# Two transformer blocks on one core: the split weight tiles get eight starting places in SBUF instead of one

## The chip, the cores and the metric

The kernel runs on one core of a Trainium2 chip (trn2). The metric is the device time of one execution in microseconds. Three executions of the kernel before took 2203.39, 2204.60 and 2204.74 us; their median is 2204.6 us.

## What is computed

Two blocks follow one another on a sequence of 256 tokens with 2048 channels, all in fp32. The first mixes a gated convolution, a pooling branch and a cross-attention to a memory of 256 tokens, and has a convolved feed-forward part; the second has a dilated and a differential attention and a feed-forward part. Nearly all the work is products of the activations with weights:

```python
def first_block(x, mem, ...):
    z = rmsnorm(x, g_mix) @ w_in                 # 2048 -> 3584, split in five
    ...                                          # conv, pooling, cross-attention
    x = x + concat([conv_out, pool_out, att]) @ w_out
    u = causal_dwconv(rmsnorm(x, g_ffn) @ w_up, ffn_conv_w) + ffn_conv_b   # 2048 -> 2 x 5632
    gate, val = split(u)
    x = x + (silu(gate) * val) @ w_down          # 5632 -> 2048
    return rmsnorm(x, g_final)

def second_block(x, ...):
    qa, ka, va, qb, kb, vb = split(rmsnorm(x, norm_attn) @ w_in)           # 2048 -> 6144
    ...                                          # two attentions of 8 heads each
    x = x + concat([ya, yb]) @ w_out
    h = rmsnorm(x, norm_ffn)
    x = x + (silu(h @ w_gate) * (h @ w_up)) @ w_down
    return rmsnorm(x, norm_final)
```

## The kernel before

**Weights in two parts.** Each fp32 number is split into two fp32r numbers: `hi` is the rounded value and `lo` the rest. A product of weight w and activation x is made as w_hi·x_hi + w_hi·x_lo + w_lo·x_hi. The activations lie as [128 channels, tile number, 512]: the 256 tokens' hi values and behind them their 256 lo values. So one weight block of 128x128 costs two matmuls: a long one, 512 columns wide, with the block's hi part as the stationary operand (`long`, L206), and a short one, 256 columns wide, with its lo part (`short`, L209). `products` runs up to four blocks at once and joins neighbouring groups, so that in steady work eight longs and eight shorts take turns. In what follows a block means one long and one short.

**Units.** The weights come in units of 16 blocks, [128, 2048] fp32, in the order of use. `prefetch` loads a unit into a `raw` tile (pool `wraw`, three tiles of 8192 bytes a partition) three units ahead. ScalarE rounds one half of it at a time into a `hi` tile (`split_hi`, L173), VectorE takes the difference into a `lo` tile (`split_lo`, L185). A half is called a part and has the number j; it holds 8 blocks in 1024 columns, 4096 bytes a partition. There are four `hi` and four `lo` tiles, used in turn. `emit_all` writes out the order by hand: per stage of four blocks it issues the prefetch, the splits, the epilogues that are due (`posts`) and then the matmuls.

**Two forms of product.** Most units run in the form above, weights stationary and activations moving (`ws_units`). For the value projections the roles are exchanged (`vs_unit`, L273 to L275): the activations' parts are stationary (128 columns of A or M), and 512 columns of a `hi` or `lo` tile are moving; there are 480 such matmuls, all 512 wide.

**Which activations.** The moving tile is `A` for the projections that start from a normalised x (`w_in`, `w_up`, gate and up, q and k), and one tile of the tag `mix` for the others: `M` (the memory, only in the first 60 us), `mix`, `hid` (the hidden values of the feed-forward part) and `y`, which lie in the same bytes one after another. 14 small blocks take theirs from the pool `qk`.

**Where tiles lie.** A pool has its place in each partition's SBUF behind the pools that were opened before it. In the order of opening, with bytes a partition: `cst`, `wraw` (3 x 8192), `whi` (4 x 4096), `wlo` (4 x 4096), `big`, `t1` (14 x 1024), `qk` (6 x 2048), `t2` (4 x 2048), and small ones. `big` holds, in the order in which its tags are first made: `X` (16384), `A` (32768), `stg` (16448, which is 16 + 16·256 floats), `mix` (32768), and four tiles of 1024 for norms. All of these sizes from `wraw` on are multiples of 512 except that of `stg`, which is 64 over one. A 128-column weight block is 512 bytes long and an activation tile's row 2048 bytes.

Of the kernel before, what the change touches and what calls it, by code (L numbers as in the profile page):

```python
# [11 lines left out]
F32R = mybir.dt.float32r  # L12
# [6 lines left out]
P = 128  # L19
# [80 lines left out]
def tile_two_blocks(ctx: ExitStack, tc: tile.TileContext, a: dict, out: bass.AP):  # L100
    nc = tc.nc
    pool = lambda name, bufs, **kw: ctx.enter_context(tc.tile_pool(name=name, bufs=bufs, **kw))
    cst = pool("cst", 1)
    wraw_p = pool("wraw", 3)
    whi_p = pool("whi", 4)
    wlo_p = pool("wlo", 4)
    big = pool("big", 1)
    t1 = pool("t1", 14)
    qk_p = pool("qk", 6)
    t2 = pool("t2", 4)  # L110
    pl_p = pool("pl", 1)
    sm = pool("sm", 4)
# [40 lines left out]

    raws = {}
    halves = {}
    HB = UB * P // 2

    def prefetch(i):
# [6 lines left out]
    def split_hi(j):  # L165

        i, second = divmod(j, 2)
        c0 = HB * second
        if i >= len(units) or c0 >= units[i][1]:
            return  # L170
        n = min(units[i][1] - c0, HB)
        hi = whi_p.tile([P, HB], F32R, tag="hi", name=f"hi{j}")
        nc.scalar.activation(hi[:, :n], raws[i][:, c0:c0 + n], AF.Copy)  # L173
        halves[j] = (hi, None)

    def split_lo(j):

        i, second = divmod(j, 2)
        c0 = HB * second
        if i >= len(units) or c0 >= units[i][1]:  # L180
            return
        n = min(units[i][1] - c0, HB)
        hi = halves[j][0]
        lo = wlo_p.tile([P, HB], F32R, tag="lo", name=f"lo{j}")
        nc.vector.tensor_tensor(out=lo[:, :n], in0=raws[i][:, c0:c0 + n], in1=hi[:, :n].bitcast(F32), op=ALU.subtract)  # L185
        halves[j] = (hi, lo)

# [293 lines left out]
    def load_mem(k0, k1):  # L481
        c = slice(KT + k0 * S if k0 else 0, KT + k1 * S)
        nc.sync.dma_start(stg[:, c], a["mem"][:, c])

    def first_units():

        n = 4 * P
        for i in range(3):
            raws[i] = wraw_p.tile([P, UB * P], F32, tag="raw", name=f"raw{i}")
            for q in range(4):  # L490
                if i != 1:
                    load_mem(2 * i + q, 2 * i + q + 1)
                nc.sync.dma_start(raws[i][:, q * n:(q + 1) * n], units[i][0][:, q * n:(q + 1) * n])

        warm = m_p.tile([P, 512], F32, tag="m", name="warm")
        for _ in range(9):
            nc.tensor.matmul(warm[:, :P], lhsT=ones, rhs=ones, start=True, stop=True)
        for j in range(4):
            hi = whi_p.tile([P, HB], F32R, tag="hi", name=f"hi{j}")
            lo = wlo_p.tile([P, HB], F32R, tag="lo", name=f"lo{j}")  # L500
            for q in range(2):
                c = slice(q * n, (q + 1) * n)
                r = raws[j // 2][:, (j % 2) * HB + q * n:(j % 2) * HB + (q + 1) * n]
                nc.scalar.activation(hi[:, c], r, AF.Copy)
                if j < 2:
                    mem_act(2 * j + q)
                nc.vector.tensor_tensor(out=lo[:, c], in0=r, in1=hi[:, c].bitcast(F32), op=ALU.subtract)
            halves[j] = (hi, lo)
# [32 lines left out]
    def mem_act(kt):  # L541
        x, g, hi = mem_t[:, kt, :], gm[:, kt:kt + 1], M[:, kt, :S]
        nc.vector.tensor_scalar(out=hi, in0=x, scalar1=g, scalar2=None, op0=ALU.mult)
        nc.vector.scalar_tensor_tensor(out=M[:, kt, S:], in0=x, scalar=g, in1=hi.bitcast(F32),
                                       op0=ALU.mult, op1=ALU.subtract)
# [183 lines left out]
    for m in LAST_TILES:  # L729
        if m < 18:  # L730
            last_blocks += full_blocks([m], act_movs, 0)
        else:
            j, ins = POOL_PAIRS[m - 18]
# [273 lines left out]
    def emit_all():  # L1007
        nc.vector.memset(ones, 1.0)
        first_units()
        n = len(units)  # L1010
        for t in range(4 * n):
            i, q = divmod(t, 4)
            if q == 0:
                prefetch(i + 3)
            if q == 2:
                split_hi(2 * i + 4)
            stage(t)
            if q == 0 and i:
                split_lo(2 * i + 2)
                split_hi(2 * i + 3)  # L1020
            elif q == 1 and i:
                split_lo(2 * i + 3)
            units[i][2](i, q)
            for fn in extras.pop(t, ()):
                fn()
        t = 4 * n
        while posts or extras or running:
            stage(t)
            for fn in extras.pop(t, ()):
                fn()  # L1030
            t += 1
        finish()
# [96 lines left out]
```

## Time and profile before

| | |
|---|---|
| median of three executions | 2204.6 us (2203.39 to 2204.74) |
| the profiled execution, its own time | 2204.54 us |
| span of its instructions, first to last | 2202.7 us |
| mean granted TensorE clock | 0.996 of 2.4 GHz |
| TensorE matmuls busy | 2182.8 us (99%), 12426 |
| TensorE weight loads busy | 1909.5 us (87%), 12426 |
| VectorE busy | 1603.5 us (73%) |
| ScalarE busy | 1143.2 us (52%) |

The profile has a page (busy times, the chain of work that ended last) and answers from the trace (groups of instructions by line and shape, a timeline in order of time, who waited for whom). A matmul's recorded length overlaps that of the next one, since matmuls are pipelined; what a matmul costs in a row of like ones is therefore read from the starts: the start of a run, the start of the next run, and the number of matmuls between them.

### The profile page before, as it was taken

The page shows a single profiled execution, that of the slowest core. Times are in us where ns is not written, and L with a number is a line of the kernel's source. Part 1 is how long each engine was busy: PE and PEld are TensorE (multiplying, and loading weights), DVE is VectorE, ACT ScalarE, POOL GpSimd, SP SyncE. Part 2 cuts the span into 40 slices and gives each one's busy share as a digit, 9 for nine tenths or more (in the row PEclk, how much of TensorE's full clock was granted, in tenths as well). Part 3 has the DMA queues.
Part 4 walks back from the last instruction along what each step waited for, and adds up shares of the span by engine and source line. Part 5 has one row for each costly group of instructions (what it writes and reads, how often), then busy time and mean ns, then how long its engine had stood idle before and what let it go on. Part 6 is the DMA issues. An engine that isn't in the chain of part 4 may idle for free.

```text
span 2202.7 us, 31334 instructions
## 1 busy us (share of the span) xinstructions
PE 2182.8 (99%) x12426; PEld 1909.5 (87%) x12426; DVE 1603.5 (73%) x2553; ACT 1143.2 (52%) x1738; POOL 106.7 (5%) x114
## 2 busy tenths in 40 slices
PE   8999999999999999999999999999999999999997
PEld 7888888888888888888888888888888888888886
DVE  8877778886588757878779677786665666666666
ACT  6555556564465536565456655464443444344442
POOL 4000010000000000003100000010000000000012
PEclk9999999999999999999999999999999999999998
DMA  7545555555555555555544444555555555555553
GB/s 285 197 169 177 191 188 193 189 192 191 191 191 186 190 182 192 188 192 188 194 167 158 161 165 153 179 203 186 185 186 192 191 189 191 191 192 186 185 184 115
DMA packets 60195, 408.99 MB, mean 186 GB/s; under 512 B 6672, under 2 KB 8592, under 8 KB 11792
## 3 DMA queue, kind: packets, MB, share of 16 engines
q1 hardware_dynamic: 60048, 406.99, 53.9%
q8 instruction: 97, 1.59, 0.3%
q14 instruction: 50, 0.41, 0.0%
HBM read 404.86 MB, written 2.10 MB: 185 GB/s over the span
## 4 chain that ended last, share of the span: by engine, by line
PE 97%; DVE 1%; DMA 1%; issue 0%; SPq 0%; ACT 0%; DVEq 0%; ACTq 0%
PE acc L206 60%; PE acc L209 31%; PE acc L273 1%; PE acc L274 1%; PE acc L275 1%; PE s_ps L430 1%; DVE lo L185 0%; DMA X<-in_x 0%; PE pT_ps L466 0%; PE o_ps L920 0%; PE o_ps L878 0%; DMA raw<-in_w_k 0%; DVE end L998 0%; PE nps L342 0%; PE o_ps L638 0%
## 5 line engine op out<-in xcount | busy, mean ns | idle before, releaser
L173 ACT ACTIVATE hi<-raw 128x1024 fp32r<-128x1024 f32 x758 | 799.2, 1057 | 583.2 <-PE acc L206 413.9
L185 DVE TENSOR_TENSOR lo<-raw,hi 128x1024 fp32r<-128x1024 f32 x758 | 933.5, 1239 | 145.4 <-ACT hi L173 133.4
L206 PE MATMUL acc<-A,hi 128*128 128x512 f32 x3776 | 961.6, 394 | 0.0
L206 PEld LDWEIGHTS acc<-A,hi 128*128 128x128 f32 x3776 | 677.3, 189 | 119.8 <-issue 1.0
L209 PEld LDWEIGHTS acc<-A,lo 128*128 128x128 f32 x3776 | 518.5, 190 | 39.2 <-issue 0.7
L209 PE MATMUL acc<-A,lo 128*128 128x256 f32 x3776 | 535.0, 283 | 0.0
L206 PE MATMUL acc<-hid,hi 128*128 128x512 f32 x1408 | 360.2, 392 | 0.0
L206 PEld LDWEIGHTS acc<-hid,hi 128*128 128x128 f32 x1408 | 250.6, 188 | 41.5
L414 ACT ACTIVATE z<-acc 128x256 f32<-128x256 f32 x244 | 91.8, 382 | 274.2 <-PE acc L206 274.1
L209 PEld LDWEIGHTS acc<-hid,lo 128*128 128x128 f32 x1408 | 195.3, 188 | 17.2
L209 PE MATMUL acc<-hid,lo 128*128 128x256 f32 x1408 | 199.6, 279 | 0.0
L740 DVE TENSOR_TENSOR X<-acc,X 128x256 f32<-128x256 f32 x128 | 54.0, 422 | 177.4 <-PE acc L206 177.3
L416 DVE TENSOR_TENSOR z<-acc,z 128x256 f32<-128x256 f32 x244 | 103.0, 422 | 103.4 <-ACT z L414 102.6
L715 DVE SCALAR_TENSOR_TENSOR c<-z,vec,c 128x255 f32<-128x255 f32 (+1 forms) x188 | 90.0, 480 | 5.1 <-ACT c L710 1.2
L404 DVE TENSOR_TENSOR hid<-hid 128x256 fp32r<-128x256 f32 x88 | 37.4, 425 | 77.1 <-ACT hid L402 77.1
L422 DVE TENSOR_TENSOR z<-z,R_ffn 128x256 f32<-128x256 f32 x176 | 74.7, 424 | 6.0
L206 PE MATMUL acc<-y,hi 128*128 128x512 f32 x256 | 65.4, 394 | 0.0
L206 PE MATMUL acc<-mix,hi 128*128 128x512 f32 x256 | 64.2, 392 | 0.0
L317 POOL TENSOR_TENSOR sq_attn<-sq_attn,sqt 128x256 f32<-128x256 f32 x30 | 29.4, 993 | 707.9 <-ACT sqt L315 707.7
L392 ACT ACTIVATE A<-X,vec 128x256 fp32r<-128x256 f32 x64 | 32.4, 507 | 57.8 <-DVE X L741 57.3
L741 DVE TENSOR_TENSOR X<-acc,X 128x256 f32<-128x256 f32 x128 | 54.3, 424 | 4.4
L395 DVE SCALAR_TENSOR_TENSOR A<-X,vec,A 128x256 fp32r<-128x256 f32 x64 | 50.6, 802 | 8.3 <-ACT A L392 8.3
(174 smaller groups left out, 1347.5 us busy)
## 6 DMA issues: line engine op xcount, KB each, us to landing
raw<-in_w_up SPq DMA_DIRECT2D x88, 1024.0 KB, 4.9
raw<-in_w_down SPq DMA_DIRECT2D x88, 1024.0 KB, 4.9
raw<-in_w_gu SPq DMA_DIRECT2D x88, 1024.0 KB, 4.9
raw<-in_w_out SPq DMA_DIRECT2D x32, 1024.0 KB, 4.9
raw<-in_w_in SPq DMA_DIRECT2D x22, 1024.0 KB, 4.9
raw<-in_w_qkb SPq DMA_DIRECT2D x16, 1024.0 KB, 4.8
raw<-in_w_qka SPq DMA_DIRECT2D x16, 1024.0 KB, 4.9
raw<-in_w_vb SPq DMA_DIRECT2D x8, 1024.0 KB, 4.8
```

The source lines that it names most:

```text
L173: nc.scalar.activation(hi[:, :n], raws[i][:, c0:c0 + n], AF.Copy)
L185: nc.vector.tensor_tensor(out=lo[:, :n], in0=raws[i][:, c0:c0 + n], in1=hi[:, :n].bitcast(F32), op=ALU.subtract)
L206: mm(acc, lhsT=hi, rhs=x, start=first, stop=last)
L209: mm(acc[:, S:], lhsT=lo, rhs=x[:, :S], start=False, stop=False)
L395: nc.vector.scalar_tensor_tensor(out=a[:, kt, S:], in0=x, scalar=g, in1=hi.bitcast(F32), op0=ALU.mult, op1=ALU.subtract)
L404: nc.vector.tensor_tensor(out=hl[:, S:], in0=src, in1=h.bitcast(F32), op=ALU.subtract)
L414: nc.scalar.activation(z, acc[:, S:], AF.Copy)
L416: nc.vector.tensor_tensor(out=z, in0=acc[:, :S], in1=z, op=ALU.add)
L422: nc.vector.tensor_tensor(out=d, in0=z, in1=R, op=ALU.mult)
L715: nc.vector.scalar_tensor_tensor(out=c[:, s:], in0=z[:, :S - s], scalar=w[2 - s], in1=c[:, s:], op0=ALU.mult, op1=ALU.add)
L740: nc.vector.tensor_tensor(out=dst, in0=acc[:, :S], in1=X[:, m, :], op=ALU.add)
L741: nc.vector.tensor_tensor(out=dst, in0=acc[:, S:], in1=dst, op=ALU.add)
```

## The change

The pools `whi` and `wlo` of four tiles become two pools of two tiles each. The first pair stays where `whi` and `wlo` were; the second pair, `whi_far` and `wlo_far`, is opened behind `qk`, so it lies behind the activations. Parts with an even number use the first pair, odd ones the second. Each tile is made 16 floats (64 bytes) longer than what is used of it. No instruction is added, removed or put in another order, and a tile is used again after four parts, as before.

```diff
     wraw_p = pool("wraw", 3)
-    whi_p = pool("whi", 4)
-    wlo_p = pool("wlo", 4)
+    whi_p = [pool("whi", 2)]
+    wlo_p = [pool("wlo", 2)]
     big = pool("big", 1)
     t1 = pool("t1", 14)
     qk_p = pool("qk", 6)
+    whi_p.append(pool("whi_far", 2))
+    wlo_p.append(pool("wlo_far", 2))
     t2 = pool("t2", 4)
...
+    def part_tile(pools, j, name):
+        return pools[j % 2].tile([P, HB + 16], F32R, tag=name, name=f"{name}{j}")[:, :HB]
...
-        hi = whi_p.tile([P, HB], F32R, tag="hi", name=f"hi{j}")
+        hi = part_tile(whi_p, j, "hi")
         nc.scalar.activation(hi[:, :n], raws[i][:, c0:c0 + n], AF.Copy)
...
-        lo = wlo_p.tile([P, HB], F32R, tag="lo", name=f"lo{j}")
+        lo = part_tile(wlo_p, j, "lo")
...
-            hi = whi_p.tile([P, HB], F32R, tag="hi", name=f"hi{j}")
-            lo = wlo_p.tile([P, HB], F32R, tag="lo", name=f"lo{j}")
+            hi = part_tile(whi_p, j, "hi")
+            lo = part_tile(wlo_p, j, "lo")
```

## Rows read from the trace of the kernel before

**Rows 1.** The page, parts 1 and 2: span, engines, granted clock in 40 slices.

```profile
span 2202.7 us, 31334 instructions
...
PE 2182.8 (99%) x12426; PEld 1909.5 (87%) x12426; DVE 1603.5 (73%) x2553; ACT 1143.2 (52%) x1738; POOL 106.7 (5%) x114
...
PEclk9999999999999999999999999999999999999998
```

**Rows 2.** The page, part 4: the chain that ended last, by engine.

```profile
PE 97%; DVE 1%; DMA 1%; issue 0%; SPq 0%; ACT 0%; DVEq 0%; ACTq 0%
```

**Rows 3.** Waits of the matmuls: who waited for whom, us, times, longest.

```profile
PE acc L274 <- DVE lo L185: 3.1, 2, 2.6
PE nps L342 <- DVE rs_y L297: 2.2, 1, 2.2
```

**Rows 4.** Groups by line and shape, matmuls: busy us, mean ns, idle before.

```profile
L206 PE MATMUL acc<-A,hi 128*128 128x512 f32 x3776 | 961.6, 394 | 0.0
L209 PE MATMUL acc<-A,lo 128*128 128x256 f32 x3776 | 535.0, 283 | 0.0
L206 PE MATMUL acc<-hid,hi 128*128 128x512 f32 x1408 | 360.2, 392 | 0.0
L209 PE MATMUL acc<-hid,lo 128*128 128x256 f32 x1408 | 199.6, 279 | 0.0
...
L273 PE MATMUL acc<-hi,A 128*128 128x512 f32 x128 | 51.2, 400 | 0.0
...
L209 PE MATMUL acc<-y,lo 128*128 128x256 f32 x256 | 35.5, 279 | 0.0
L209 PE MATMUL acc<-mix,lo 128*128 128x256 f32 x256 | 35.1, 278 | 0.0
```

**Rows 5.** Timeline of matmuls, moving tile A: start, us, line, how many in a row.

```profile
1760.05 2.00 PE L206 MATMUL acc<-A,hi 128*128 128x512 f32 x8
1761.89 1.12 PE L209 MATMUL acc<-A,lo 128*128 128x256 f32 x8
1762.84 2.00 PE L206 MATMUL acc<-A,hi 128*128 128x512 f32 x8
1764.68 1.11 PE L209 MATMUL acc<-A,lo 128*128 128x256 f32 x8
...
1771.22 1.09 PE L206 MATMUL acc<-A,hi 128*128 128x512 f32 x4
```

**Rows 6.** The same timeline, moving tile hid.

```profile
1704.38 2.00 PE L206 MATMUL acc<-hid,hi 128*128 128x512 f32 x8
1706.21 1.07 PE L209 MATMUL acc<-hid,lo 128*128 128x256 f32 x8
1707.12 1.99 PE L206 MATMUL acc<-hid,hi 128*128 128x512 f32 x8
1708.95 1.11 PE L209 MATMUL acc<-hid,lo 128*128 128x256 f32 x8
1709.89 2.00 PE L206 MATMUL acc<-hid,hi 128*128 128x512 f32 x8
```

**Rows 7.** Timeline, hi and lo moving, blocks of A stationary: 12 matmuls apart.

```profile
1074.22 0.39 PE L273 MATMUL acc<-hi,A 128*128 128x512 f32 x1
...
1076.94 0.39 PE L273 MATMUL acc<-hi,A 128*128 128x512 f32 x1
```

**Rows 8.** Timeline, hi and lo moving, blocks of M stationary: 23 matmuls apart.

```profile
17.90 0.39 PE L273 MATMUL acc<-hi,M 128*128 128x512 f32 x1
...
23.26 0.40 PE L275 MATMUL acc<-hi,M 128*128 128x512 f32 x1
```

**Rows 9.** Groups by line and shape, ScalarE's and VectorE's splits and two small VectorE operations.

```profile
L173 ACT ACTIVATE hi<-raw 128x1024 fp32r<-128x1024 f32 x757 | 798.3, 1057 | 583.2 <-PE acc L206 413.9 <-issue 94.5 <-PE acc L275 37.8
...
L185 DVE TENSOR_TENSOR lo<-raw,hi 128x1024 fp32r<-128x1024 f32 x757 | 932.5, 1240 | 145.4 <-ACT hi L173 133.4
...
L741 DVE TENSOR_TENSOR X<-acc,X 128x256 f32<-128x256 f32 x128 | 54.3, 424 | 4.4
...
L822 DVE TENSOR_TENSOR X<-X,sq_attn 128x256 f32<-128x256 f32 x16 | 6.1, 414 | 0.0
```

## The prediction

> **What bounds the kernel now.** Read the busy times first, then the chain, the waits, and at last the starts of the matmuls. TensorE's matmuls are busy for 2182.8 of 2202.7 us and the granted clock is full in 39 of 40 slices [rows 1]. The chain that ended last is TensorE for 97% [rows 2], and its matmuls wait for almost nothing: the longest entry is 3.1 us in all [rows 3]. So no wait can be shortened. The time is the number of matmuls times the step from one start to the next, and an edit matters only if it changes that step. The recorded lengths (394 and 283 ns) overlap and are not the step; the timeline gives it.
>
> With A moving, eight longs go from 1762.84 to 1764.68, 230.0 ns each, and eight shorts start at 1761.89 and end at 1762.84, 118.8 ns each; 32 blocks from 1760.05 to 1771.22 make 349.1 ns a block [rows 5]. With hid moving, longs take 1.83/8 = 228.8 ns, and shorts either 0.91/8 = 113.8 or 0.94/8 = 117.5, taking turns; 16 blocks from 1704.38 to 1709.89 make 344.4 ns a block [rows 6]. Shapes, clock and lines are the same. The groups say it over the whole run: a short's mean is 283 ns with A, 279 with hid and y, 278 with mix [rows 4]. In the exchanged form the step is 2.72/12 = 226.7 ns with blocks of A stationary [rows 7] and 5.36/23 = 233.0 with blocks of M [rows 8]. So one shape has steps that differ by 3%, with no wait in any of them, and what differs is the tile that is read.
>
> **Where the tiles lie.** From the sizes in the code, modulo 512 bytes and counted from the first hi tile: before, all hi and lo tiles and A lie at 0, and M, mix, hid and y at 64, since stg is 64 bytes over. So part minus activation is 0 with A and -64 with the mix tag. In the exchanged form stationary minus moving is 0 with A and +64 with M. The three distances have the three prices above. That a weight load and the moving stream get in each other's way when both read SBUF, and that the distance modulo 512 sets how often, is my inference; the trace shows only that distance and step go together.
>
> After: hi of even parts at 0 and 64, lo at 128 and 192, A at 256 (four tiles of 4160 bytes before it), the mix tag at 320, hi of odd parts at 320 and 384, lo at 448 and 512, that is 0 again. These are seven places, not eight. The distances, in the order of parts 0, 2, 1, 3: with A, hi 256, -192, 64, 128 and lo -128, -64, 192, 256; with the mix tag, hi 192, 256, 0, 64 and lo -192, -128, 128, 192.
>
> **The change part by part.** Nothing is added, removed or reordered, and a tile is reused after four parts as before, so no queue is passed and no wait is added. What moves is the addresses, with two possible costs.
>
> *The splits.* ScalarE's 757 splits of 1057 ns and VectorE's 757 of 1240 ns now write elsewhere. ScalarE stands idle 583.2 us before its splits, 413.9 of it waiting for matmuls to free a tile [rows 9]: TensorE hides it. VectorE is busy 1603.5 of 2202.7 us [rows 1]. The nearest rows for a price are two VectorE operations of 128x256, one on tiles at one place (424 ns), one on tiles 64 apart (414) [rows 9]: 10 ns or 2.4%. On 932.5 us of splits that is 22 us either way, inside some 600 us of idle VectorE. I take nothing. Were the cover gone, it would cost up to 22 us.
>
> *The matmuls' steps.* Counts [rows 4]: 3776 blocks with A; 1408 + 256 + 256 = 1920 with hid, y and mix; 384 exchanged ones with A. (M and the pool's tiles, some 80 blocks, and 96 exchanged ones with M are left out; half a per cent on them is 0.2 us.) Bounds for a distance that the trace does not show: below, the cheapest long and short seen, 226.7 + 113.8 = 340.5 ns a block; above, the dearest, 233.0 + 118.8 = 351.8. If all were at the lower end, the gain is 3776 x 8.6 + 1920 x 3.9 = 32.5 + 7.5 = 40 us, giving 2164.5. If all were at the upper end, the loss is 3776 x 2.7 + 1920 x 7.4 + 384 x 6.3 = 10.2 + 14.2 + 2.4 = 27 us, giving 2231.3.
>
> Between them I choose by the nearest rows: a distance that is an odd multiple of 64 is priced as the mix tag is now (344.4), an even one as A is now (349.1), since these are the only two classes with both matmuls shown. By the list above exactly half of the parts are odd and half even, with A and with the mix tag. So both kinds of block come to (349.1 + 344.4)/2 = 346.7. With A: 3776 x -2.35 = -8.9 us. With the mix tag: 1920 x +2.35 = +4.5. The exchanged ones are at the best step now, 226.7, and half of them go to 233.0: 384 x 3.15 = +1.2. Sum -3.2 us.
>
> The sum is made against the profiled execution's 2204.5 us (span 2202.7 and 1.8 around it); the median of the runs is 2204.6, the same. Forecast: 2201.3 us. Anything within 0.2% (2200.1 to 2208.9) is about what a measurement of this kernel cannot tell from no change.
>
> **The rivals.**
>
> *Faster: only near distances cost.* If a load disturbs the stream only when it lies within 64 bytes of it modulo 512, then 128, 192 and 256 are free. With A one of four distances stays near for hi and one for lo: the long becomes 0.75 x 226.7 + 0.25 x 230.0 = 227.5, the short 0.75 x 113.8 + 0.25 x 117.5 = 114.7, the block 342.2, -6.9 x 3776 = -26.1 us. With the mix tag half of hi is near and no lo: (226.7 + 229.4)/2 + 113.8 = 341.9, -2.5 x 1920 = -4.8. Time 2173.6. For it: A's shorts are near the dearest seen, and they are most of the shorts. Against it: distance 0 has the cheapest long [rows 7], so near is not simply bad. Chance 0.25.
>
> *Slower: being ahead costs.* A stationary block 64 ahead of the moving row has 233.0 [rows 8], 64 behind it 228.8 [rows 6]. If every distance from +64 to +256 has the first price and, for shorts, 118.8 against a mean of 115.6 behind, then with A three of four hi are ahead: 0.75 x 233.0 + 0.25 x 228.8 = 231.9, and two of four lo: 117.2, together 349.1 as now, 0 us. With the mix tag three hi are ahead and one at 0: 0.75 x 233.0 + 0.25 x 230.0 = 232.3, and two of four lo: 117.2, which is 349.5 against 344.4, +5.1 x 1920 = +9.8. Half of the exchanged ones are ahead: +1.2. Time 2204.5 + 11.0 = 2215.5. It decides once the mean block exceeds today's (3776 x 349.1 + 1920 x 344.4)/5696 = 347.5 ns. For it: every long that is cheapest now is at 0, which only a quarter of the hi parts keep, and only with the mix tag. Chance 0.25.
>
> *Nothing: the change doesn't do what it says.* A lies in one stretch of SBUF and the mix tag in another, so the stretch, not the place modulo 512, may set the step; then parts behind the activations and padding change nothing, 2204.5. Against it: the exchanged form takes its moving data from the same hi and lo tiles in [rows 7] and [rows 8], and the order low/high of the two tiles is the same in both. The Trainium skill would agree with this rival. "TensorE: Matmul & The Clock Gate", section "Step-by-step: what each phase is for", says that loading the next tile's weights takes no SBUF read bandwidth from the running matmul, and "SBUF — State Buffer", section "Who interferes with whom", that TensorE waits on nobody; by that the places could not matter. The trace, with 226.7 and 233.0 ns for one shape, does not bear that out, unless something else than the reads makes the difference. Chance 0.12.
>
> **How the numbers follow.** Forecast 0.38, with a range of its own from 2195 to 2208; it lies so near the edge of what can be told that I give 0.15 of it to faster, 0.21 to same and 0.02 to slower. Faster rival 0.25, slower rival 0.25, nothing 0.12. So faster 0.40, same 0.33, slower 0.27. The range of 8 in 10 leaves out the far parts of the two rivals and the two bounds: 2178 to 2222.
>
> **What would show it.** In the profile after: shorts with A between 114 and 119 ns by part, no longer one value; with hid and mix about half the parts dearer than now; the exchanged ones with A no longer all at 226.7; no new waits on TensorE; the splits' means within 2.4%. If shorts with A come to 114 throughout, the faster rival holds; if longs come to 232 and more, the slower one; if the steps stay at 349.1 and 344.4, nothing was done. It would be wrong altogether if VectorE's splits grew enough that matmuls wait for lo tiles.

## The result, and the profile after

| | before | after |
|---|---|---|
| median of four executions | 2204.67 us | 2217.47 us (2217.06 to 2217.98) |
| ratio, with its 95% interval | | 1.0059 (1.0042 to 1.0077) |
| profiled execution | 2204.54 us | 2217.66 us |
| span | 2202.7 us | 2215.9 us |

The change makes the kernel slower by 12.8 us, 0.6%. The forecast was 2201.3 us, 3.2 us faster; the measured time lies inside the range (2178 to 2222), but on the other side of no change.

The page after, span, engines, granted clock and chain, answers to [rows 1] and [rows 2]:

```profile
span 2215.9 us, 31334 instructions
...
PE 2195.7 (99%) x12426; PEld 1911.8 (86%) x12426; DVE 1604.3 (72%) x2553; ACT 1143.5 (52%) x1738; POOL 106.1 (5%) x114
...
PEclk9999999999999999999999999999999999999998
...
PE 97%; DVE 1%; DMA 1%; issue 0%; SPq 0%; ACT 0%; DVEq 0%; ACTq 0%
```

Same instructions, same clock, same chain. VectorE and ScalarE are as busy as before, TensorE's matmuls 12.9 us longer. The waits of the matmuls (us in all, times, longest) and the splits, as [rows 3] and [rows 9]; the lines of the code have moved by 8:

```profile
PE acc L282 <- DVE lo L193: 3.9, 2, 2.7
PE nps L350 <- DVE rs_y L305: 2.2, 1, 2.2
...
L193 DVE TENSOR_TENSOR lo<-raw,hi 128x1024 fp32r<-128x1024 f32 x757 | 932.1, 1239 | 149.2 <-ACT hi L181 137.5
L181 ACT ACTIVATE hi<-raw 128x1024 fp32r<-128x1024 f32 x757 | 798.9, 1058 | 590.7 <-PE acc L214 427.3 <-issue 95.8 <-PE acc L283 36.6
```

No wait has come up and the splits take 1058 and 1239 ns, as before. What has changed is the step. The timeline of matmuls after, with A moving (L214 long, L217 short; start, us, line, how many), as [rows 5]:

```profile
1762.27 2.03 PE L214 MATMUL acc<-A,hi 128*128 128x512 f32 x8
1764.13 1.10 PE L217 MATMUL acc<-A,lo 128*128 128x256 f32 x8
1765.07 2.03 PE L214 MATMUL acc<-A,hi 128*128 128x512 f32 x8
1766.93 1.11 PE L217 MATMUL acc<-A,lo 128*128 128x256 f32 x8
...
1770.69 2.02 PE L214 MATMUL acc<-A,hi 128*128 128x512 f32 x8
```

and with hid moving, as [rows 6]:

```profile
1709.11 2.02 PE L214 MATMUL acc<-hid,hi 128*128 128x512 f32 x8
1710.96 1.11 PE L217 MATMUL acc<-hid,lo 128*128 128x256 f32 x8
1711.91 2.01 PE L214 MATMUL acc<-hid,hi 128*128 128x512 f32 x8
...
1714.68 1.99 PE L214 MATMUL acc<-hid,hi 128*128 128x512 f32 x8
1716.50 1.13 PE L217 MATMUL acc<-hid,lo 128*128 128x256 f32 x8
...
1720.27 1.09 PE L214 MATMUL acc<-hid,hi 128*128 128x512 f32 x4
```

With A, eight longs take 1.86 us where they took 1.84, and 24 blocks from 1762.27 to 1770.69 are 350.8 ns each (349.1 before). With hid, 32 blocks from 1709.11 to 1720.27 are 348.8 ns each (344.4 before); runs of longs differ from one to the next (1.85, then 1.82 us). The mean steps over all starts of each trace (steps over 260 ns left out, which are the few waits) are:

| ns | long | short | block | time |
|---|---|---|---|---|
| A before | 230.4 | 119.3 | 349.7 | |
| A after | 232.0 | 119.2 | 351.1 | 3776 x +1.4 = +5.3 us |
| mix tag before | 229.4 | 116.2 | 345.7 | |
| mix tag after | 230.9 | 118.3 | 349.2 | 1920 x +3.5 = +6.7 us |
| exchanged with A, before / after | 228.0 / 230.6 | | | 384 x +2.6 = +1.0 us |

The sum is 13.0 us of the 13.1 between the two profiled executions. So the whole loss is in the steps. The places of the tiles stand in no view of the profile; they follow from the sizes in the code, and by these there are seven of them modulo 512, not the eight of the title.

### The profile page after: what moved, and what is told of

The parts are those of the page before. It is cut to its first block, busy times and chain, and to the rows that moved or that the text cites. A ratio compares the mean times of both kernels' runs of the same rounds, so it can differ in the third digit from the quotient of the medians.

```text
span 2215.9 us, 31334 instructions
## 1 busy us (share of the span) xinstructions
PE 2195.7 (99%) x12426; PEld 1911.8 (86%) x12426; DVE 1604.3 (72%) x2553; ACT 1143.5 (52%) x1738; POOL 106.1 (5%) x114
## 4 chain that ended last, share of the span: by engine, by line
PE 97%; DVE 1%; DMA 1%; issue 0%; SPq 0%; ACT 0%; DVEq 0%; ACTq 0%
PE acc L214 60%; PE acc L217 31%; PE acc L281 1%; PE acc L282 1%; PE acc L283 1%; PE s_ps L438 1%; DMA raw<-in_w_k 1%; DVE lo L193 0%; PE pT_ps L474 0%; PE o_ps L928 0%; PE o_ps L886 0%; DVE M L551 0%; DVE end L1006 0%; DVE M L552 0%; PE nps L350 0%
## 5 line engine op out<-in xcount | busy, mean ns | idle before, releaser
L181 ACT ACTIVATE hi<-raw 128x1024 fp32r<-128x1024 f32 x758 | 799.7, 1058 | 590.7 <-PE acc L214 427.3
L193 DVE TENSOR_TENSOR lo<-raw,hi 128x1024 fp32r<-128x1024 f32 x758 | 933.1, 1239 | 149.2 <-ACT hi L181 137.5
L214 PE MATMUL acc<-A,hi 128*128 128x512 f32 x3776 | 967.5, 395 | 0.0
L214 PEld LDWEIGHTS acc<-A,hi 128*128 128x128 f32 x3776 | 675.3, 188 | 121.8 <-issue 1.0
L217 PEld LDWEIGHTS acc<-A,lo 128*128 128x128 f32 x3776 | 518.1, 188 | 43.9 <-issue 0.7
L217 PE MATMUL acc<-A,lo 128*128 128x256 f32 x3776 | 534.2, 282 | 0.0
L214 PE MATMUL acc<-hid,hi 128*128 128x512 f32 x1408 | 362.2, 393 | 0.0
L214 PEld LDWEIGHTS acc<-hid,hi 128*128 128x128 f32 x1408 | 250.9, 188 | 42.7
L217 PEld LDWEIGHTS acc<-hid,lo 128*128 128x128 f32 x1408 | 197.6, 188 | 18.0
L217 PE MATMUL acc<-hid,lo 128*128 128x256 f32 x1408 | 202.2, 281 | 0.0
L214 PE MATMUL acc<-y,hi 128*128 128x512 f32 x256 | 65.8, 395 | 0.0
L214 PE MATMUL acc<-mix,hi 128*128 128x512 f32 x256 | 64.6, 393 | 0.0
```

The source lines that it names most:

```text
L214: mm(acc, lhsT=hi, rhs=x, start=first, stop=last)
L217: mm(acc[:, S:], lhsT=lo, rhs=x[:, :S], start=False, stop=False)
```

## The experiments

**Do the place, the stretch or the mixture count?** The first theory after the result was that each distance has its own step (place). Its rivals: lying behind the activations costs (stretch), or the changes of distance from part to part cost (mixture).

*e1: half behind, one place.* The changed kernel without its padding, with a filler that keeps the old distances.

```diff
-        return pools[j % 2].tile([P, HB + 16], ...)[:, :HB]
+        return pools[j % 2].tile([P, HB], ...)
...
+    pool("gap", 1).tile([P, 112], F32, name="gap")
     whi_p.append(pool("whi_far", 2))
```

> Half of the hi and lo tiles lie behind the activations, as in the changed kernel, but without the 64 bytes of padding and with a filler of 448 bytes, so that all of them keep distance 0 to A and -64 to the mix tag, as before. Theory 'place' (only the distance modulo 512 bytes counts, each distance having its own step) and theory 'mixture' (a change of distance from part to part costs): 2204.6 us, A's long and short at 230.4 and 119.4 ns. Theory 'stretch' (lying behind the activations costs): 2217 us.

Measured: 2204.43 us, ratio 1.0001 (0.9992 to 1.0010). Lying behind the activations costs nothing; the theory 'stretch' is out.

*e2: spread, all in front.* The kernel before with each hi and lo tile 64 bytes longer (`HB + 16`, of which `HB` is used).

> All eight tiles stay in front of the activations, each 64 bytes longer: with A the distances are hi 0, 64, 128, 192 and lo 256, -192, -128, -64, with the mix tag 64 less. Theory 'stretch': 2204.6 us. Theory 'place', with the mean step of each distance as the changed kernel's trace shows it (long 230.4, 233.0, 231.7, 229.5; short 119.7, 115.3, 120.4, 118.8): about 2212 us. Theory 'mixture': as the changed kernel, 2217 us.

Measured: 2214.56 us, ratio 1.0047 (1.0032 to 1.0062). The spread alone costs most of what the change costs; the time lies between the numbers of 'place' and 'mixture' and doesn't decide between them.

*e3 and e4: one distance, another one.* The kernel before with a filler between the lo tiles and the activations, of 256 bytes (64 floats) and of 448 (112 floats).

```diff
+    pool("gap", 1).tile([P, 64], F32, name="gap")     # e3; 112 in e4
     big = pool("big", 1)
```

> The tiles are those of the kernel before, with a filler of 256 bytes between the lo tiles and the activations: one distance, 256, with A, and 192 with the mix tag. Theory 'place', with the changed kernel's means for these distances (long 230.3 and 229.5, short 119.7 and 118.6): about 2210 us. Theory 'mixture': a single distance settles, so both kinds of block come below the changed kernel's means, 2205 us or less. Theory 'stretch': 2204.6 us.

> As the run before, with a filler of 448 bytes: one distance, +64, with A, and 0 with the mix tag. Theory 'place': with the mix tag what A has now (230.4 and 119.4 ns), with A a long of 233.0 and a short of some 118.8: about 2219 us. Theory 'mixture': the steps of the two tiles change places at most, 2205 to 2212 us. Theory 'stretch': 2204.6 us.

Measured: e3 2204.60 us, ratio 1.0003 (0.9993 to 1.0012), e4 2203.85, ratio 1.0000 (0.9991 to 1.0010). By the times all single distances would seem alike. The groups by line and shape of e3 (line, busy us, mean ns of one) tell more:

```profile
L207 PE MATMUL acc<-A,hi 128*128 128x512 f32 x3776 | 961.6, 394 | 0.0
L210 PE MATMUL acc<-A,lo 128*128 128x256 f32 x3776 | 534.9, 283 | 0.0
L207 PE MATMUL acc<-hid,hi 128*128 128x512 f32 x1408 | 360.2, 392 | 0.0
L210 PE MATMUL acc<-hid,lo 128*128 128x256 f32 x1408 | 199.6, 278 | 0.0
```

These are the numbers of [rows 4] to within 0.1 us. The steps over the whole trace are also the same, 230.4 and 119.3 ns with A, 229.5 and 116.3 with the mix tag. So 256 is as good as 0, and 192 as -64: distances count modulo 256, not 512. In e4 the steps change:

```profile
L207 PE MATMUL acc<-A,hi 128*128 128x512 f32 x3776 | 970.2, 396 | 0.0
L210 PE MATMUL acc<-A,lo 128*128 128x256 f32 x3776 | 517.6, 278 | 0.0
```

A, now at +64, has 232.7 and 114.8 ns, 2.2 less a block; the mix tag, now at 0, has 230.5 and 119.0, which is what A had, 3.8 more. 3776 x -2.2 and 1920 x +3.8 cancel by chance. Where there is one distance all along, each has its own step.

**What is the price of each distance?** A settled price is the mean step in a kernel that has one distance all along (later: one for all hi tiles and one for all lo tiles). With prices at 0, +64 and -64 this theory, 'settled price', could be put to the test: put A at the cheapest of them.

*e5: one distance of 128.* A filler of 128 bytes (`[P, 32]`) as in e3.

> One distance again, -128 with A and -192 with the mix tag, which is +64 modulo 256; the run before showed that 256 and 0 have the same steps, and 192 and -64. Theory 'settled price' (one distance all along settles, with a price a block by distance modulo 256: 349.7 ns at 0, 347.5 at +64, 345.7 at -64): the mix tag at 347.5 ns a block, +3.6 us; A's price at 128 is not known: 2204 to 2208 us if it lies among the others, and if the slowdown of the spread tiles is all due to it (theory 'place'), 357 ns a block and 2236 us.

Measured: 2217.86 us, ratio 1.0061 (1.0046 to 1.0076), above the range and short of the other time given. The groups with A:

```profile
L207 PE MATMUL acc<-A,hi 128*128 128x512 f32 x3776 | 970.2, 396 | 0.0
L210 PE MATMUL acc<-A,lo 128*128 128x256 f32 x3776 | 533.6, 282 | 0.0
```

A at 128 has 232.6 and 119.0, 351.7 ns a block, the dearest of the four; the mix tag at -192 has 232.7 and 115.1, like A at +64 in e4. 3776 x 2.0 + 1920 x 2.1, and 1.6 for the exchanged products at 232.3, make 13.2 us.

*e6: -64 for both.*

```diff
+    pool("gap", 1).tile([P, 16], F32, name="gap")
     big = pool("big", 1)
...
-    stg = big.tile([P, KT + KT * S], F32, tag="stg", name="mem")
+    stg = big.tile([P, KT + KT * S + 112], F32, tag="stg", name="mem")
...
```

> One distance of -64 with A and with the mix tag (a filler of 64 bytes in front of the activations, stg lengthened by 448 bytes). Theory 'settled price': A's blocks come from 349.7 to 345.7 ns, 3776 x 4.0 = -15.1 us, the exchanged products with A go from 228 to 233 ns, +2 us: 2191 us. Theory 'all single distances are alike': 2204 us.

Measured: 2191.18 us, ratio 0.9939 (0.9924 to 0.9954), as the settled prices say. The groups with A, which before had 394 and 283 ns:

```profile
L207 PE MATMUL acc<-A,hi 128*128 128x512 f32 x3776 | 957.1, 393 | 0.0
L210 PE MATMUL acc<-A,lo 128*128 128x256 f32 x3776 | 523.7, 279 | 0.0
```

and its timeline with A, which now is that of [rows 6], with shorts of 0.90 and 0.95 us a run by turns:

```profile
1760.58 2.00 PE L207 MATMUL acc<-A,hi 128*128 128x512 f32 x8
1762.42 1.07 PE L210 MATMUL acc<-A,lo 128*128 128x256 f32 x8
1763.32 1.99 PE L207 MATMUL acc<-A,hi 128*128 128x512 f32 x8
1765.15 1.11 PE L210 MATMUL acc<-A,lo 128*128 128x256 f32 x8
1766.10 2.00 PE L207 MATMUL acc<-A,hi 128*128 128x512 f32 x8
...
1771.61 1.08 PE L207 MATMUL acc<-A,hi 128*128 128x512 f32 x4
```

32 blocks in 11.03 us, 344.7 ns each. The one size that was worse, the exchanged products at 233.3 ns, is as [rows 8] had it.

**Do changes between parts cost?** *e7 and e8* give each of the four hi and lo tiles a pool of its own with a pad behind it, all in front of the activations. The diff is against the changed kernel; what it removes is left out.

```diff
+    PADS = (16, 112, 16, 112)      # e7: places 0, 64, 0, 64;  e8: (0, 16, 0, 112), places 0, 0, 64, 64
+    whi_p = [pool(f"whi{j}", 1) for j in range(4)]
+    wlo_p = [pool(f"wlo{j}", 1) for j in range(4)]
...
+        return pools[j % 4].tile([P, HB + PADS[j % 4]], F32R, tag=name, name=f"{name}{j}")[:, :HB]
```

> The four hi and four lo tiles lie at 0, 64, 0, 64 in the order of use, a hi and its lo alike: with A the distances 0 and +64, with the mix tag -64 and 0. Theory 'place' with settled prices: half of the blocks at each, (349.7 + 347.5)/2 with A and (345.7 + 349.5)/2 with the mix tag, 2204 us, as the next run. Theory 'mixture': a cost at each change of distance, 2210 to 2217 us.

> The same two places in the order 0, 0, 64, 64: the same share of blocks at each distance as the run before, with half as many changes of distance. Theory 'place': 2204 us, as the run before. Theory 'mixture': half of the run before's excess over 2204 us.

Measured: e7 2213.47 us, ratio 1.0042 (1.0025 to 1.0059); e8 2209.83, ratio 1.0026 (1.0017 to 1.0036). The shares at each distance are the same, and with half the changes the excess over the 2204.3 us of the kernel before is 5.5 us instead of 9.2. So a change between parts costs here: A's block has 350.4 ns in e7 and 349.8 in e8 where the settled prices give 348.6. The same is seen in e2: the settled prices of its four distances give about 2207 us, 348.6 ns a block with A, and 2214.56 us and 350.2 ns were measured.

The trace of e8 shows where the cost lies. Shorts come eight to a part; those from 1759.04 are of the first part at +64 behind two at 0, those from 1761.85 of the second, those from 1764.62 of the next part at 0 (counted in the order of use):

```profile
1759.04 1.10 PE L214 MATMUL acc<-A,lo 128*128 128x256 f32 x8
1759.98 2.03 PE L211 MATMUL acc<-A,hi 128*128 128x512 f32 x8
1761.85 1.08 PE L214 MATMUL acc<-A,lo 128*128 128x256 f32 x8
1762.77 2.01 PE L211 MATMUL acc<-A,hi 128*128 128x512 f32 x8
1764.62 1.12 PE L214 MATMUL acc<-A,lo 128*128 128x256 f32 x8
1765.57 2.00 PE L211 MATMUL acc<-A,hi 128*128 128x512 f32 x8
```

They take 0.94, 0.92 and 0.95 us. Over the whole trace A's shorts at +64 have 117.9 ns in the first part behind the change and 115.8 in the second; in e4, with no change, they have 114.8, and in e7, where every part at +64 comes behind one at 0, 118.1. So a short's price at a distance depends also on the part before, and the settled prices alone don't give the time of a mixed kernel.

**Does the short's price depend on where the long's load lies?** In the changed kernel lo lies 128 bytes on from hi in every part, so a short's lo never lies at the distance of its hi.

*e9: hi at -64, lo at +64; e10: hi 0, lo 128 with A.* A filler of 128 bytes between hi and lo tiles in both, then one in front of the activations.

```diff
+    pool("gap1", 1).tile([P, 32], F32, name="gap1")
     wlo_p = pool("wlo", 4)
+    pool("gap", 1).tile([P, 48], F32, name="gap")     # e9, with the longer stg of e6; 32 and stg as it was in e10
     big = pool("big", 1)
```

> One distance for all hi tiles, -64, and one for all lo tiles, +64, modulo 256, with A and the mix tag alike: the cheapest long seen (229.3 ns) beside the cheapest short (114.9). Theory 'long and short are priced apart': 344.2 ns a block, A's -5.5 x 3776 and the mix tag's -1.5 x 1920, exchanged products +1.5: 2182 us. Theory 'a load at another distance than the one before it disturbs the next': shorts or longs dearer than these, 2187 us and more.

> One distance for all hi tiles and one for all lo tiles, lo 128 bytes on from hi as in the changed kernel, but the same in every part: with A hi 0 and lo 128, with the mix tag hi -64 and lo +64. Theory 'priced apart': 349.4 ns a block with A, 344.4 with the mix tag, 2200.7 us. If what the changed kernel's shorts have above their settled prices (1.4 ns with A, 0.9 with the mix tag) comes from the difference between hi and lo and not from the changes between parts: 2208 us.

Measured: e9 2186.64 us, ratio 0.9920 (0.9905 to 0.9935); e10 2211.93, ratio 1.0034 (1.0021 to 1.0047). Neither is the sum of prices taken apart. In e10 A's shorts have 120.6 ns, with no change anywhere between parts; with hi at 128 too they had 119.0. In e9 the longs of a run have 228.8 (229.0 in e6), but the last one of each run, during which the first lo of the next run is loaded, has 235.5, against 230.2 in e6. So the place of the tile that is loaded during a matmul counts for its step. It doesn't set it alone: with lo at 0 that last long has 227.7 in the kernel before, where hi is at 0, and 235.0 in e13 below, where hi is at 128. Even so e9 is the fastest kernel of all, 17.8 us below the one before. Its timeline with A, all shorts now at 0.91 us a run:

```profile
1759.91 2.00 PE L208 MATMUL acc<-A,hi 128*128 128x512 f32 x8
1761.74 1.07 PE L211 MATMUL acc<-A,lo 128*128 128x256 f32 x8
1762.65 2.00 PE L208 MATMUL acc<-A,hi 128*128 128x512 f32 x8
...
1770.89 2.00 PE L208 MATMUL acc<-A,hi 128*128 128x512 f32 x8
```

32 blocks in 10.98 us, 343.1 ns each.

*e13: hi 128, lo 0 with A; hi +64, lo -64 with the mix tag.* The filler between hi and lo alone. With e9 and e10, every pair of the changed kernel has then been run by itself, though (+64, -64) with the mix tag only and (0, 128) with A only.

> One distance for all hi tiles and one for all lo tiles, with A hi 128 and lo 0, with the mix tag hi +64 and lo -64: the two pairs of the changed kernel that no run has had alone. Theory 'pairs' (the changed kernel's excess is the settled price of its pairs of hi and lo distances): the steps of the changed kernel's own parts of these pairs, long 232.8 and short 119.7 ns with A, 232.3 and 118.3 with the mix tag, 2225 us. Theory 'changes' (the excess comes from the change between parts): the steps that runs with equal distances had, short 119.4 with A and 116.4 with the mix tag, 2220 us.

Measured: 2217.47 us, ratio 1.0057 (1.0040 to 1.0073), below both numbers. With the mix tag the short has 118.1 ns, as 'pairs' had it (118.3) and not the 116.4 of equal distances. With A it has 117.9, which neither theory gave.

**Is it the distance, and how fine is it?** *e11* is e6 with a filler of 32 bytes in front of the raw tiles (`[P, 8]`); *e12* and *e14* are e6 with 8 and 24 floats in place of 16, distances -32 and -96.

> As e6, with every tile from the raw ones on moved by 32 bytes, so that rows start at a multiple of 64 bytes. Only distances count: 2191 us, as e6. If the start within 64 bytes counts: another time, the sign open.

> As e6, with a distance of -32 bytes in place of -64, with A and the mix tag. If the price runs evenly between 0 and -64: 347.6 ns a block, 2200 us. If 64 bytes are the grain: the steps of one of the two, 2208 or 2191 us.

> One distance of -96 bytes with A and the mix tag. After 345.6 ns a block at -64 and 350.5 at -32: if odd multiples of 32 are dear, 350 ns a block and 2214 to 2218 us; if the price falls or rises evenly to the 351.7 ns at 128, 348.7 and 2206 us.

Measured: e11 2190.22 us, ratio 0.9935 (0.9919 to 0.9952), as e6: of the start itself nothing is seen, the distance counts. e12 2217.27, ratio 1.0059 (1.0044 to 1.0074), dearer than any number given; e14 2237.05, ratio 1.0145 (1.0129 to 1.0160), the slowest of all, also beyond both numbers given and beyond the 2231.3 us that the prediction had taken for the dearest. The groups of e14 with A:

```profile
L207 PE MATMUL acc<-A,hi 128*128 128x512 f32 x3776 | 971.9, 396 | 0.0
L210 PE MATMUL acc<-A,lo 128*128 128x256 f32 x3776 | 538.8, 283 | 0.0
```

All settled prices, part minus activation modulo 256, in ns:

| hi, lo | long | short | block | from |
|---|---|---|---|---|
| -64, +64 | 229.7 | 114.9 | 344.6 | e9, A |
| -64, -64 | 229.2 | 116.4 | 345.6 | e6, A |
| +64, +64 | 232.7 | 114.8 | 347.5 | e4, A |
| 0, 0 | 230.4 | 119.3 | 349.7 | before, A |
| -32, -32 | 233.3 | 117.2 | 350.5 | e12, A |
| +64, -64 | 232.4 | 118.1 | 350.5 | e13, mix tag |
| 128, 0 | 232.7 | 117.9 | 350.6 | e13, A |
| 0, 128 | 230.7 | 120.6 | 351.3 | e10, A |
| 128, 128 | 232.6 | 119.0 | 351.7 | e5, A |
| -96, -96 | 233.2 | 120.6 | 353.8 | e14, A |

## Why the prediction was wrong

**Right.** What bounds the kernel: no wait came up, the splits took no longer (1058 and 1239 ns; the price that the prediction had for their places compared unlike rows, since L741 reads `acc` from PSUM, but nothing hung on it), and the steps of the matmuls alone carry the result. That the distance of part and activation counts for the step, which the prediction called an inference from three cases, is now shown: e1 keeps the distances and changes the stretch, 2204.4 us; e11 keeps them and moves all tiles, as e6; e6 and e14 change them by 32 bytes and lie 46 us apart. The rival 'nothing' is out: with some 9 us of waits on TensorE in e9 and in e14, the same instructions took 2187 and 2237 us by their operands' places. The Trainium skill says in "SBUF — State Buffer", section "Who interferes with whom", that TensorE waits on nobody. Read as that rival read it, that the places could not matter, it isn't borne out for these products; that it is the reads of SBUF that collide is not shown either.

**The step that failed** is the price of the distances not seen: an odd multiple of 64 was priced as the mix tag was, an even one as A was. It gave 346.7 ns a block for both tiles; measured were 351.1 with A and 349.2 with the mix tag. Most of the miss is with A, where -8.9 us were forecast and +5.3 came. +64 is not priced as -64: its long has 232.7 ns, not 229.2 (e4, e6). 128 is not priced as 0: its long has 232.6, not 230.4 (e5). The trace of before held a warning: the exchanged products had 233.0 at +64 where the longs at -64 had 228.8; the prediction used both and still gave +64 and -64 one price. And modulo 512 should have been 256 (e3), which makes the seven places four distances.

**The second fault** was to leave out that hi and lo of a part lie at different distances from the activation: the forecast priced a block by whether its distances are odd or even, and both rivals priced hi and lo apart. With the prices of single distances and this done, A would have 349.9 ns a block (long 232.1, short 117.8) and the mix tag 348.1. Priced by pairs, from the table: A's four parts are (0, 128), twice (+64, -64), (128, 0), a long of 232.0 and a short of 118.7, 350.7 ns; the mix tag's are (-64, +64), twice (0, 128), (+64, -64), 349.7 with the mix tag's own prices where there are such (230.2 and 115.4 in e10). That is 3776 x 1.0 + 1920 x 4.0 + 1.0 = 12.5 us of the 13.1. Measured were 351.1 and 349.2, so for changes between parts there remain +0.4 and -0.5 ns, under 1 us together. These two partly cancel, and two of the pairs were priced with the other tile. Part by part the changed kernel's trace says much the same: its shorts have 118.3 and 118.3 ns with A at (+64, -64) and 118.2 with the mix tag (118.1 alone), 115.3 at (-64, +64) (115.4), 120.4 with A at (0, 128) (120.6). Off are A's shorts at (128, 0), 119.7 for 117.9, and the mix tag's at (0, 128), 119.6 where A alone had 120.6.

**The rivals.** 'Slower' had 2215.5 us, 2 us from the result, but its rule is only half borne out. Longs at +64 and 128 are dear (232.7, 232.6), as it said. Distances of 192 are -64 and cheap, and a short at +64 is the cheapest there is (114.8), where the rule had 118.8. Its A block was 349.1 (351.1 measured), its mix block 349.5 (349.2): the time agrees in part by errors that cancel. 'Faster' falls: 128, which it took to be free, is the dearest of the multiples of 64.

**What stays open.** Why distances have these prices was not tried; the table is an observation, and that loads and moving stream get in each other's way stays the prediction's inference. Nor is it settled why changes between parts cost 1.8 and 1.2 ns a block with A in e7 and e8, and 1.6 in e2, where hi and lo keep equal distances, and next to nothing in the changed kernel. Spreading the parts also moves what ScalarE and VectorE write against what TensorE reads meanwhile, and no run separates that from the changes. Why A at (128, 0) has a short of 117.9 alone and 119.7 in the changed kernel belongs to the same question.

## What to carry to other kernels

Where a kernel is a dense stream of matmuls with no waits, read the steps from the starts, group by the tile that is read, and look for steps that differ at the same shape. Then try single distances between weight and activation tiles with a filler of a few bytes, one run each, rather than spreading the tiles: a spread loses the cheap price, and the three spreads that kept hi and lo alike (e2, e7, e8) were 5 to 9 us above the mean of their prices besides. Two unknown distances aren't priced alike because both are odd multiples of something; measure each, and hi and lo together.

## What the runs showed of the hardware

For 128x512 and 128x256 fp32r matmuls with a weight load each, the mean step of a kernel with one distance for all hi tiles and one for all lo tiles goes by the distance of stationary and moving operand modulo 256 bytes: 229 to 233 ns and 115 to 121 ns. Where distances change from part to part, it depends also on the part before (a short at +64: 114.8 ns, 117.9 behind a change in e8). Fillers of at most 448 bytes moved this kernel from 2186.6 to 2237.1 us (2.3%) without a change to any instruction but its addresses. Distances of -32 and -96 were dearer than -64 between them (350.5, 353.8 and 345.6 ns a block), so the price does not run evenly.
